# Cross attention in seven products: order of pairs in the second pass, raw buffers, loads two products ahead, and FFN combinations in three steps

## The chip, the core and the metric

The kernel runs on one core of one Trainium2 chip, as one program. The metric is the device time of one execution in microseconds; lower is better. The engines are TensorE (PE, with its weight loads PEld), VectorE (DVE), ScalarE (ACT), GpSimd (POOL) and SyncE (SP), which here issues most of the transfers. POOL issues transfers too.

## The reference

One step of a streaming encoder layer over 2048 prompt rows (16 tiles of 128) and 128 sample rows, model width 1024. Three sub-layers stand in sequence, each with a norm before and after it and its result added to the residual:

- a mixer: 8 heads of chunked band attention and a depthwise convolution side by side, one projection in and one out (`y = concat([att, c]) @ w_out`);
- cross attention: 4 heads of 256 into 256 memory rows (`softmax(q @ mk.T / 16) @ mv @ w_mo`, with `q = h @ w_mq`);
- a SwiGLU FFN: `(silu(h @ w_gate) * (h @ w_up)) @ w_down`, hidden width 2816.

The outputs are the rows of both groups and the new caches. All is computed to float32 accuracy.

## The kernel before, in words

**Precision.** Each float32 operand is split into a rounded part and a rest ("hi" by an ACT cast, "lo" by a subtraction on DVE or POOL), and each product is three matmuls, `hi*hi + hi*lo + lo*hi` (`mm3`, lines 290 to 294; the three lines are L292, L293, L294).

**Stages.** Memory keys and values, input projections, band attention, output projection (`mixout`, with the sample rows' cross attention spread between its matmuls), prompt cross attention (`phase_cross`), gate and up (`gate_up`), down (`down`).

**Cross attention.** The query and key weights are folded into one 1024x1024 matrix f1 (scores = h times f1), and value and output weights into f2. Pass one (q = 0 to 7) multiplies by f1 and takes the softmax, whose rows go to a DRAM array `zs`; pass two (q = 8 to 15) multiplies the `zs` rows by f2. Each q is a pair of row tiles. The two tiles of a pair and the four quarters of the matrix form a 2x2 block product, done in seven products instead of eight, in the order 0, 1, 3, 4, 5, 6, 2. Each product is 12 matmuls of 128x512 into one PSUM bank. Line 1488 stands in the loop over q and the seven products.

For a pair, `left` loads two tiles (of x1 in pass one, normed; of `zs` in pass two) into the two `xt` buffers, `turned` transposes them on TensorE and makes four sums on POOL (L1372 to L1375), `split` makes hi and lo rows (L1380, L1381), and `collect` adds the products into two z tiles (L1445 is the first copy, L1447 to L1458 the sums). The z region holds four tiles, two pairs. In pass one `softmax` follows (L1387 to L1394). In pass two `residual` follows when a tile's sum is ready: x1 is loaded (L1466), the row is normed (L1339 on ACT, L1341 and L1342 on POOL, L1398 on DVE), x1 is added (L1399, POOL) and the result is stored as x2 (L1400). For the first three pairs (group g = 0) the FFN norm follows (L1404) and `combine` (L1410 to L1417): four sums on POOL and four stores to `hn`, the left operands of the FFN's own seven products. These are the "FFN pairs".

`form` loads a half of one of the seven weight combinations into a `raw` buffer (L1327, SP) and splits it (L1330, L1332). The combined quarters are made earlier by `quad` and wait in `comb`. In pass one the loads stand in `form` itself, `AHEAD` products ahead; at q = 7 the same places are filled with f2.

**Gate and up.** `tform` loads `hn` pieces into `nat` buffers (L1537), transposes them (L1540) and splits them (L1542, L1543). `wforms` loads two weight blocks into `wf`, makes four sums on POOL (L1557 to L1560) with results in `s`, and splits seven forms (L1562, L1563). A block of f does seven products of 12 matmuls of 384 columns; there are 22 blocks for each of three groups, and every second block (odd f) ends with `act_forms`, four more POOL sums. In the first group, `natural` prepares the `hn` of the other eight pairs, one pair each in an odd block: two loads, two norms, one `combine`, all in one call. It has six jobs, two for a pair of half height among them.

**Sample rows in the output projection.** `mixout` does 17 tiles; from the third on every second of the eight steps of a tile adds `RATE` to a counter, and for each whole one a step of `cross_sample` is run (65 in all):

```
due += RATE if i >= FROM else 0.0
while due >= 1:
    next(fill, None)
```

**Places.** Tiles are given fixed places in a few big tiles (`sbF`, `sbR`, the PSUM tile; `Region.at`, offsets in KB) and in smaller ones that are released from phase to phase ("flexb" in the profile). A tag with several places rotates through them. Whoever takes a place waits for the last reader of what was there.

**Order.** Each engine and each queue runs its instructions in a fixed order. The framework plans that order in advance (`schedule_with_timeline_sim=True`, line 1841): the program's order gives the priority, raised for the first forms of `gate_up` by `high_priority(offset=HP)`, and a cost model says when an instruction could start. A wait holds up all that stands behind it on its queue.

## Time and profile before

| | us |
|---|---|
| runs | 3067.57, 3067.44, 3058.28 (median 3067.44) |
| profiled execution, its own time | 3062.37 |
| span of the profile | 3060.6 |
| granted TensorE clock, mean | 0.974 |
| TensorE busy | 2933.8 (96%) |
| VectorE busy | 2282.2 (75%) |
| GpSimd busy | 1618.8 (53%) |
| ScalarE busy | 1446.4 (47%) |

Times in the profile are microseconds from the start of the span. A row of a timeline gives the start, the length, the engine, the line, the operation, output and inputs, the count, and in brackets how long the engine had been idle before it and what ended that. "SPq" and "POOLq" are the queues' own instructions. A busy TensorE is not a TensorE at full rate: its granted clock falls when it has stood idle, so work done is better read from the number of matmuls in a stretch.

### The profile page before, as it was taken

Reading aid. Unit: us, or ns where it says so; the run is one execution under the profiler, and the core shown is the slowest. Engines: PE = TensorE matmul, PEld = TensorE weight load, DVE = VectorE, ACT = ScalarE, POOL = GpSimd, SP = SyncE. Lnnn points to the kernel's source line nnn. Section 1 sums busy time; section 2 is a strip of 40 time slices with the busy share of each in tenths; the row PEclk is TensorE's granted clock in tenths of the full one; section 3 lists DMA queues with packets and bytes.
Section 4 is the critical chain, followed back from the end, with each engine's and each line's share of the span. In section 5 each row is a group of like instructions: output and inputs, shape, how many; then the busy total and the mean of one; then the engine's idle time right before and its main releaser. Section 6 shows DMA issues by size and latency. Waiting matters only on the chain.

```text
span 3060.6 us, 46528 instructions
## 1 busy us (share of the span) xinstructions
PE 2933.8 (96%) x16748; PEld 2696.8 (88%) x16748; DVE 2282.2 (75%) x3224; ACT 1446.4 (47%) x2903; POOL 1618.8 (53%) x1488
## 2 busy tenths in 40 slices
PE   9999999999999997999777899999999999999998
PEld 9999999989987886787667899999999999888887
DVE  6686987867775566778567898887878998665666
ACT  5444455668773344555324333443334444433433
POOL 0267595711125435868766765555555776523413
PEclk9999999989999998999888999999999999999999
DMA  7645252654436656545457443354425334766664
GB/s 273 240 148 170 94 180 93 217 204 168 180 121 220 240 194 205 190 145 193 154 185 237 162 149 130 145 179 162 155 105 175 144 139 172 259 198 200 217 231 146
DMA packets 212500, 544.68 MB, mean 178 GB/s; under 512 B 20710, under 2 KB 86126, under 8 KB 203429
## 3 DMA queue, kind: packets, MB, share of 16 engines
q1 hardware_dynamic: 192733, 455.33, 43.7%
q0 software_dynamic: 19536, 86.39, 7.5%
q8 instruction: 131, 2.15, 0.3%
q14 instruction: 100, 0.82, 0.1%
HBM read 393.76 MB, written 158.58 MB: 180 GB/s over the span
## 4 chain that ended last, share of the span: by engine, by line
PE 71%; DVE 7%; POOL 7%; DMA 7%; issue 6%; ACT 2%; SPq 0%; POOLq 0%; DVEq 0%; ACTq 0%
PE psb L294 18%; PE psb L293 18%; PE psb L292 18%; PE psb L300 5%; PE psb L908 2%; PE psb L878 2%; DMA sbf<-in_w_down_dram 2%; PE psb L895 2%; POOL sbf L1685 1%; DVE flexb L1381 1%; DVE sbr L1563 1%; POOL sbf L1399 1%; DMA sbf<-in_w_in_dram 1%; PE psb L1540 1%; PE psb L841 1%
## 5 line engine op out<-in xcount | busy, mean ns | idle before, releaser
L292 PE MATMUL psb<-sbr 128*128 128x384 f32 (+3 forms) x2808 | 942.2, 337 | 11.1 <-DVE sbf L1622 3.7
L293 PE MATMUL psb<-sbr 128*128 128x384 f32 (+3 forms) x2356 | 805.9, 342 | 0.4 <-DVE sbr L342 0.3
L294 PE MATMUL psb<-sbr 128*128 128x512 f32 (+3 forms) x1848 | 634.6, 345 | 3.2 <-DVE sbr L1755 3.1
L292 PEld LDWEIGHTS psb<-sbr 128*128 128x128 f32 x2808 | 530.1, 189 | 41.7 <-DVE sbf L1622 4.1
L294 PE MATMUL psb<-sbr,sbx 128*128 128x384 f32 (+2 forms) x1484 | 475.8, 322 | 0.2 <-POOL sbx L287 0.2
L293 PEld LDWEIGHTS psb<-sbr 128*128 128x128 f32 x2356 | 445.1, 189 | 26.8 <-DVE sbr L342 0.5
L294 PEld LDWEIGHTS psb<-sbr 128*128 128x128 f32 x1848 | 349.0, 189 | 33.0 <-DVE sbr L1755 6.1
L1563 DVE TENSOR_TENSOR sbr<-sbf,sbr 128x512 fp32r<-128x512 f32 x258 | 267.9, 1040 | 40.5 <-ACT sbr L1562 39.0
L1562 ACT CAST sbr<-sbf 128x512 fp32r<-128x512 f32 x258 | 159.3, 620 | 269.6 <-PE psb L293 224.5
L294 PEld LDWEIGHTS psb<-sbr,sbx 128*128 128x128 f32 x1484 | 279.7, 189 | 0.8 <-POOL sbx L287 0.5
L546 DVE SCALAR_TENSOR_TENSOR psb<-sbf,psb 128x768 f32<-128x768 f32 (+1 forms) x290 | 264.4, 912 | 6.1
L1755 DVE TENSOR_TENSOR sbr<-sbf,sbr 128x384 fp32r<-128x384 f32 (+2 forms) x242 | 175.4, 748 | 91.9 <-ACT sbr L1754 90.2
L292 PE MATMUL psb<-sbr,flexb 128*128 128x512 f32 (+2 forms) x528 | 199.8, 379 | 20.6 <-ACT sbf L1445 16.0
L287 POOL TENSOR_TENSOR sbx<-sbf,sbr 128x1024 fp32r<-128x1024 f32 (+1 forms) x62 | 153.0, 2470 | 89.2 <-ACT sbr L285 85.8
L294 PE MATMUL psb<-sbr,flexb 128*128 128x512 f32 (+2 forms) x528 | 198.5, 377 | 0.2 <-DVE flexb L1563 0.2
L1685 POOL TENSOR_TENSOR sbf<-sbf 128x512 f32<-128x512 f32 x77 | 107.7, 1404 | 167.1 <-DMA sbf<-in_w_down_dram 165.4
L293 PE MATMUL psb<-sbr,flexb 128*128 128x512 f32 (+2 forms) x500 | 190.5, 381 | 3.1 <-DVE sbr L1332 2.2
L1754 ACT CAST sbr<-sbf 128x384 fp32r<-128x384 f32 (+2 forms) x242 | 112.5, 483 | 171.2 <-PE psb L293 144.7
L556 POOL TENSOR_TENSOR flexb<-flexb,flexb 128x128 f32<-128x128 f32 (+1 forms) x180 | 168.8, 938 | 25.8 <-ACT flexb L555 15.5
L1562 ACT CAST sbx<-sbf 128x512 fp32r<-128x512 f32 x153 | 94.7, 620 | 177.9 <-PE psb L293 148.0
L1563 DVE TENSOR_TENSOR sbx<-sbf,sbx 128x512 fp32r<-128x512 f32 x153 | 159.2, 1041 | 22.1 <-ACT sbx L1562 21.8
L292 PE MATMUL psb<-sbr,sbx 128*128 128x384 f32 (+1 forms) x524 | 170.8, 328 | 2.5 <-ACT sbr L1542 2.0
(379 smaller groups left out, 6902.1 us busy)
## 6 DMA issues: line engine op xcount, KB each, us to landing
af<-flexb SPq DMA_DIRECT2D x33, 1344.0 KB, 5.9
sbf<-in_w_down_dram SPq DMA_DIRECT2D x154, 256.0 KB, 3.8
sbf<-in_w_gate_dram SPq DMA_DIRECT2D x66, 512.0 KB, 3.3
sbf<-in_w_up_dram SPq DMA_DIRECT2D x66, 512.0 KB, 3.4
sbf<-af SPq DMA_DIRECT2D x85, 384.0 KB, 3.8
sbf<-x SPq DMA_DIRECT2D x51, 512.0 KB, 4.7
sbf<-in_w_in_dram SPq DMA_DIRECT2D x48, 512.0 KB, 3.6
sbr<-ks POOLq DMA_DIRECT2D x16, 1024.0 KB, 7.6
```

What stands on the lines that cost most here:

```text
L287: self.lo_engine.tensor_tensor(lo[:, c], wf[:, c], hi[:, c].bitcast(F32), ALU.subtract)
L292: nc.tensor.matmul(ps, lh, rh, start=start, stop=False, **kw)
L293: nc.tensor.matmul(ps, lh, rl, start=False, stop=False, **kw)
L294: nc.tensor.matmul(ps, ll, rh, start=False, stop=stop, **kw)
L300: nc.tensor.matmul(y[o], l, r[:, o * 512:(o + 1) * 512], start=start and x == 0, stop=stop and x == 2)
L546: nc.vector.scalar_tensor_tensor(acc if w < CW - 1 else o, src(w), cwt[:, j, w:w + 1], acc, ALU.mult, ALU.add)
L556: nc.gpsimd.tensor_tensor(o, o, v, ALU.add)
L1562: nc.scalar.copy(hs[j][:, :], src[j])
L1563: nc.vector.tensor_tensor(ls[j][:, :], src[j], hs[j][:, :].bitcast(F32), ALU.subtract)
L1685: nc.gpsimd.tensor_tensor(acc[:, :], acc[:, :], q[:, :], ALU.add if s > 0 else ALU.subtract)
L1754: nc.scalar.copy(ch[:, m], a[:, x, m])
L1755: nc.vector.tensor_tensor(cl[:, m], a[:, x, m], ch[:, m].bitcast(F32), ALU.subtract)
```

## The change

Constants: `RATE` 1.1 becomes 1.25, `AHEAD` 2 becomes 3, `POOLED` (the products whose second "lo" is made on POOL) loses all of pass one and has three products instead of four in pass two, and `VORDER` gives the order of the pairs in pass two. In `phase_cross` the raw loads leave `form` and are issued two products ahead of it; their places, and those of the PSUM tags, are listed anew; the next pair's `left(1)` stands behind the first forms; the x1 loads of pass two leave `collect` and SP, and are issued on POOL's queue at the fourth product of a pair; the post gain is loaded at the sixth product of q = 7. `natural` becomes a generator with three steps (loads and sums of squares; scaling; combination), of which one runs after each block of the first group, and its places move. `gate_up` gets other places for nearly all its tiles: the weights (`wf`) where the g tiles of cross attention were, `nat` where `xt` was, the forms where the forms of the first products were.

```
-RATE = 1.1
+RATE = 1.25
-AHEAD = 2
-POOLED = ((3, 4, 5, 6, 2), (0, 3, 5, 2))
+AHEAD = 3
+POOLED = ((), (4, 6, 2))
+VORDER = (3, 0, 4, 1, 5, 2, 6, 7)
...
-                .at("raw", 4, (sbF, [16, 20, 24, 28]), *[(a, o) for _ in range(2) for a, o in (
-                    (ft, [0]), (fx, [0]), (sbF, [46.5, 24, 28]))], *[(a, o) for _ in range(5) for a, o in (
-                        (ft, [0]), (fx, [0]), (sbF, [46.5]))])
+                .at("raw", 4, (sbF, [16, 20, 24, 28, 16, 20, 24, 28, 46.5]), (ft, [0]), (sbF, [24, 28]), (fx, [0]), (sbF, [46.5]),
+                    *[(a, o) for _ in range(4) for a, o in ((ft, [0]), (fx, [0]), (sbF, [46.5, 42.5]))])
...
-        ps_mm = ps_t = Region().at("mm", 2, (self.ps, [0, 2, 4, 6])).at("t", 2, (self.ps, [12, 14, 8, 10]))
+        ps_mm = ps_t = Region().at("mm", 2, (self.ps, [2, 6, 0, 4])).at("t", 2, (self.ps, [8, 10, 12, 14]))
+        turn = lambda q: pairs[q] if q < 8 else pairs[VORDER[q - 8]]
...
-        def form(m, j):
+        def raw(m, j):
             out = []
-            for a in range(2):
-                raw = self.t(pool, [P, 2, 512], F32, "raw")
...
+                out.append(self.t(pool, [P, 2, 512], F32, "raw"))
+                nc.sync.dma_start(out[-1][:, :, :], src)
+            return out
+
+        def form(m, j, parts):
+            out = []
+            for a, x in enumerate(parts):
...
-            for t in pairs[q % 8][:2]:
+            for t in turn(q)[:2]:
...
-        late = Region().lay(sbF, 0, ("na", 4, 1), ("nb", 4, 1), ("nt", 4, 1))
-        def natural(g, p):
...
+        late = (Region().at("na", 4, (sbF, [16])).at("nb", 4, (sbF, [20])).at("nt", 4, (sbF, [46.5]))
+                .at("junk", 2, (sbF, [34.5])).lay(sbF, 50.5, ("ss", 0.015625, 6), ("rstd", 0.015625, 6)))
+        def naturals(jobs):
+            for g, p in jobs:
+                n = PAIRS[g][p][2]
+                out = []
+                for tag, (t, r0) in zip(("na", "nb"), PAIRS[g][p][:2]):
+                    x = self.t(late, [P, D], F32, tag)[:n, :]
+                    nc.sync.dma_start(x, self.x2[t][r0:r0 + n, :])
+                    out.append((x, rstd(x, n, late)))
+                yield
+                for x, r in out:
+                    stt(x, x, r[:n, :], gffn[:n, :], ALU.mult, ALU.mult)
+                yield
+                combine(self.hn[g][:, p, :, :], *[x for x, _ in out], self.t(late, [P, 2, 512], F32, "nt")[:n])
+                yield
+        self.todo = naturals([(1, 0), (1, 1), (1, 2), (2, 0), (2, 1), (2, 2)])
...
-                x = self.t(pool, [P, D], F32, "x1")[:, :]
-                nc.sync.dma_start(x, self.x1[t])
+                x = xs.pop((q, "b" if j == 5 else "a"))
                 residual(t, y, x)
...
         nat = left(0)
+        raws = [raw(0, j) for j in order[:2]]
         gs = turned(nat)
         acts = {j: split(*gs[j]) for j in order}
-        nat = left(1)
         f = {}
         for x in range(AHEAD):
-            f[order[x]] = form(0, order[x])
+            f[order[x]] = form(0, order[x], raws.pop(0))
+            raws.append(raw(0, order[x + 2]))
+        nat = left(1)
         for q in range(16):
             for x, j in enumerate(order):
                 if q == 0 and x + AHEAD < 7:
-                    f[order[x + AHEAD]] = form(0, order[x + AHEAD])
+                    f[order[x + AHEAD]] = form(0, order[x + AHEAD], raws.pop(0))
+                    if x + AHEAD + 2 < 7:
+                        raws.append(raw(0, order[x + AHEAD + 2]))
...
+                if q == 6 and x in (2, 4):
+                    raws.append(raw(1, order[x // 2 - 1]))
                 if q == 7:
-                    f[j] = form(1, j)
+                    f[j] = form(1, j, raws.pop(0))
+                    if x + 2 < 7:
+                        raws.append(raw(1, order[x + 2]))
+                    if x == 5:
+                        self.gpost = self.gain(pool, "g_mem_post", "gain")
+                if q > 7 and x == 3:
+                    for t, name in zip(turn(q), "ab"):
+                        xs[q, name] = self.t(pool, [P, D], F32, "x1")[:, :]
+                        nc.gpsimd.dma_start(xs[q, name], self.x1[t])
...
-            if q == 7:
-                self.gpost = self.gain(pool, "g_mem_post", "gain")
...
-        pool = (Region().at("wf", 4, (sbF, [12, 18, 46.5, 22]))
-                .at("s", 2, (sbF, [26, 28, 38.5])).at("nat", 2, (sbF, [40.5, 42.5, 44.5]))
...
+        pool = (Region().at("wf", 4, (sbF, [0, 4, 8, 12]))
+                .at("s", 2, (sbF, [42.5, 44.5, 24])).at("nat", 2, (sbF, [40.5, 38.5, 36.5]))
...
-                .at("wh", 2, (sbR, [68, 72, 76, 80, 84, 88, 92, 104]), (w8, [0]))
+                .at("wh", 2, (sbR, [100, 104, 64, 80, 84, 68, 0, 4]), (w8, [0]))
...
-        for j, (oh, ol) in enumerate(((0, 6), (12, 18), (56, 62), (24, 30), (36, 42), (48, 96))):
+        for j, (oh, ol) in enumerate(((88, 94), (8, 14), (20, 26), (72, 32), (38, 44), (50, 56))):
...
-                    if g == 0 and x == 1 and self.todo:
-                        self.natural(*self.todo.pop(0))
+                    if g == 0:
+                        next(self.todo, None)
```

34 lines of the change are left out of this document (11 added, 23 removed).

## The prediction

> **What bounds the kernel now.** I read the page first, then the busy time by stage, then the idle gaps of TensorE with what ended them, then the rows of the queue that ended each.
>
> ```profile
> PE 2933.8 (96%) x16748; PEld 2696.8 (88%) x16748; DVE 2282.2 (75%) x3224; ACT 1446.4 (47%) x2903; POOL 1618.8 (53%) x1488
> ```
>
> TensorE is the bound over the whole span, so an edit that leaves its instructions alone can only win back time in which it stood or ran slowly. The busy time by stage (start:end, length, PE busy, instructions, granted clock) shows where:
>
> ```profile
> 1187.70:1240.00 52.30, 32.70 (x129) 0.77 0.52 171
> 1240.00:1390.00 150.00, 147.24 (x695) 1.00 0.52 179
> 1390.00:1470.00 80.00, 77.42 (x369) 0.98 0.50 175
> 1470.00:1550.00 80.00, 56.12 (x230) 0.81 0.47 172
> 1550.00:1592.20 42.20, 42.20 (x189) 1.00 0.48 160
> 1592.20:1680.00 87.80, 57.74 (x321) 0.83 0.68 231
> 1680.00:1800.00 120.00, 106.28 (x577) 0.94 0.49 170
> 1800.00:1950.00 150.00, 150.00 (x867) 1.00 0.33 122
> ```
>
> Cross attention runs from 1187.7 to 1592.2, gate and up after it. Undisturbed, a matmul of cross attention costs 0.226 us (42.2 us for 189, four of them transposes) and one of gate/up 0.173 us (150/867). The transposes within the stages, busy time and count:
>
> ```profile
> 1187.70:1240.00 52.30, 6.86 (x44) 0.77 0.52 171
> 1240.00:1390.00 150.00, 13.20 (x100) 1.00 0.52 179
> 1470.00:1550.00 80.00, 6.72 (x37) 0.81 0.47 172
> 1592.20:1680.00 87.80, 15.42 (x88) 0.83 0.68 231
> ```
>
> At 0.132 us each (13.20/100) the full-rate work is: stage A (1187.7 to 1240) 44×0.132 + 85×0.226 = 25.0; stage D (1470 to 1550) 41×0.132 + 189×0.226 = 48.1 (37 transposes and four of the next phase); stage E (1592.2 to 1680) 88×0.132 + 233×0.173 = 51.9; stage F (1680 to 1800) 577×0.173 = 99.8. Lost: **A 27, D 32, E 36, F 20 us**, and some 5 us in the rest of cross attention (150 − 147.24 and 80 − 77.42 idle). Those 120 us are all that the change can reach. The gaps on TensorE, the idle time in brackets:
>
> ```profile
> 1201.16 0.76 PE L292 MATMUL psb<-sbx,flexb 128*128 128x512 f32 x1 [9.00 <-DVE flexb L1081]
> 1475.59 0.79 PE L292 MATMUL psb<-sbr,flexb 128*128 128x512 f32 x1 [5.48 <-ACT sbf L1445]
> 1514.20 0.80 PE L292 MATMUL psb<-sbr,flexb 128*128 128x512 f32 x1 [9.32 <-ACT sbf L1445]
> 1611.23 1.97 PE L1540 MATMUL psb<-ident,sbf 128*128 128x128 f32 x8 [19.02 <-DMA sbf<-hn]
> 1742.70 0.69 PE L292 MATMUL psb<-flexb,sbx 128*128 128x384 f32 x1 [6.31 <-DVE flexb L1613]
> ```
>
> **The change part by part.**
>
> *Start of cross attention (A).* The 9.00 us go to the new PSUM order: the first product now takes the bank of the output projection's last tile but one, not one that L1081 of the last tile still reads. The rest is late raw loads on SP (a row of its queue, and the landing of L1327's loads):
>
> ```profile
> 1215.01 0.90 SPq L1327 DMA_DIRECT2D flexb<-comb  x2
> ...
> DMA to landing us min/median/max: 3.3/3.5/7.2
> ```
>
> The flexb pair at 1215, 27 us into the phase, is the third product's; these two buffers come free only when the last mixer tile is stored. Now the third and fourth products use 16 to 31 KB of the big tile again, and the two flex buffers first serve the second half of the fifth and the seventh. RATE 1.25 finishes the sample stream's 65 steps by step 52 of 60 (1.25×52 = 65) instead of step 60 (1.1×60 = 66), so buffers that the first forms need are free two tiles earlier. The subtractions of pass one leave POOL:
>
> ```profile
> L1332 DVE TENSOR_TENSOR sbr<-sbf,sbr x6: 1214/1220/3378, 1182.4 to 1406.6; 128x1024 fp32r<-128x1024 f32 x6
> L1332 POOL TENSOR_TENSOR sbr<-sbf,sbr x4: 2364/2963/3454, 1184.2 to 1388.2; 128x1024 fp32r<-128x1024 f32 x4
> ```
>
> Five of 2.96 us become five of 1.22 on DVE, 6.1 us more there. What is late next: the flex buffer, and a mixer tail without filler. The chain of the tile before the last shows both (squares, residual sum, store, and the landing of such stores):
>
> ```profile
> 1173.24 0.59 ACT L1077 ACTIVATE flexb<-psb 128x512 bf16<-128x512 f32 x1
> 1178.09 3.31 POOL L1082 TENSOR_TENSOR flexb<-flexb 128x1024 f32<-128x1024 f32 x1 [0.69 <-DVE flexb L1081]
> 1182.60 0.62 POOL L1083 DMA_DIRECT2D x<-flexb  x1
> ...
> DMA to landing us min/median/max: 3.1/5.8/7.9
> ```
>
> From the squares to the residual sum, which follows the last read of PSUM, 4.8 us: with the sample's matmuls gone, two tile boundaries stand open for up to that, 9.6 us; transposes of the first pair can fill some, I take 6. From squares to the store's issue 10 us, landing 3.1 to 5.8; then a raw load of 3.5, a cast of about 1 and a subtraction of 1.2 (its DVE row): the fifth product's second half is ready 19 to 22 us after the tile, needed after 4.5 products of 12×0.226 = 2.7, at 12. That is some 9 us of stall. DVE has two forms of 1.2 a product of 2.7, beside splits and collecting: another 5, an estimate. A costs 20 instead of 27: **7 saved**; bounds −5 (POOL and DVE hold the tile's tail as long as now, and 9.6 of tail less the 5 of forms come on top) and 22 (only the 5 of forms stay).
>
> *Second pass (D).* TensorE waits for ACT's first copy of a pair, which waits for a z buffer, freed when a pair two before is normed and stored. That is late because x1 is late:
>
> ```profile
> 1460.20 31.04 SPq L1355 DMA_DIRECT2D sbf<-zs  x4
> 1491.35 0.36 SPq L1466 DMA_DIRECT2D sbf<-x  x1
> 1495.62 2.40 POOL L1399 TENSOR_TENSOR sbf<-sbf 128x1024 f32<-128x1024 f32 x1 [2.67 <-DMA sbf<-x]
> ```
>
> L1355 stands on SP for buffers that TensorE's transposes free, with x1's load queued behind: 31 us. Now x1 leaves SP for POOL's queue, issued at the fourth product. POOL pays two issues per pair; the nearest row is that of its stores, and beside it stand the other prices of POOL (busy, mean ns):
>
> ```profile
> L1400 POOL DMA_DIRECT2D x<-sbf x16: 533/605/628, 1423.5 to 1608.9; - x16
> ...
> L1342 POOL TENSOR_TENSOR sbf<-sbf,mhalf 128x1 f32<-128x1 f32 x23 | 14.8, 646 | 1.3
> L1373 POOL TENSOR_TENSOR sbf<-sbf 128x512 f32<-128x512 f32 x7 | 10.6, 1511 | 0.3
> L1341 POOL TENSOR_SCALAR sbf<-sbf 128x1 f32<-128x1 f32 x23 | 10.4, 453 | 22.0 <-ACT sbf L1339 21.1
> ```
>
> POOL's work for a pair: four sums of 1.5, two residuals of 2.4, two rstd of 1.1 (0.45 + 0.65), two stores of 0.6: 14.2; an FFN pair adds two rstd, four combinations of 1.5 and four stores: 24.8. TensorE's pair is 84×0.226 + 16×0.132 = 21.1. Three FFN pairs in a row overrun it by 3.7 us each; alternated with plain ones, two pairs with the new issues cost 41.4 of 42.2. So the new order balances POOL, with hardly any slack. What queues behind a waiting x1 load on POOL: the sums of the pair after next, which the splits and then TensorE wait for. An x1 buffer of a plain pair is free only when the FFN pair's combinations have landed, a wait of 3 to 6 us (L1083's landing), three times. So 15 remain of 32: **17 saved**; bounds −76 (the slow rival's price) and 29.
>
> The Trainium skill (SBUF — State Buffer, "SBUF: two separate sides") speaks against this step: a DMA of the GpSimd queue cannot write its descriptors while DVE holds the shared port pair, some 3.1 us in place of 0.62. By that the 16 loads would cost up to 40 us of POOL; the trace disagrees so far, since L1400's 16 issues never exceed 628 ns.
>
> *Loads two ahead, q=6 and 7.* POOL's forms go from four to three; the gap here is 2 us in 1390 to 1470. Nothing taken; −3 to 3.
>
> *Into gate/up (E).* Before, the hn loads wait for the region of the post gain, freed by the last L1398:
>
> ```profile
> 1595.79 1.26 POOL L1414 TENSOR_TENSOR sbf<-sbf 128x512 f32<-128x512 f32 x1
> 1601.27 0.19 POOL L1341 TENSOR_SCALAR sbf<-sbf 128x1 f32<-128x1 f32 x1
> 1604.92 1.28 DVE L1398 SCALAR_TENSOR_TENSOR sbf<-sbf 128x1024 f32<-128x1024 f32 x1
> ```
>
> L1398 ends at 1606.2, 14 us after the last product, about 5 of them because L1341 stands behind a combination burst on POOL. Now hn lands in the old xt buffers and the weights in the g buffers, both idle for most of the last pair, so the first four activation forms are done under it. What is late next: the weight sums (L1557) go into the gain's region. From the last product, an estimate: L1398 ends at about 8 us (14 less POOL's 5 and some), then come two POOL sums of 1.3, a cast and a subtraction of under 1 each: product two starts near 12, while TensorE has 12×0.173 = 2.1 us of product and 36 transposes (4.8). Some 5 us stand open; with DVE and POOL busy and the clock lagging after it (0.83 in this stage) I take 16 left of 36: **20 saved**; bounds 8 (transposes and forms stay late, less than half of the 19 goes) and 32.
>
> *Naturals in three steps (F).*
>
> ```profile
> 1737.78 4.40 DVE L1563 TENSOR_TENSOR sbr<-sbf,sbr 128x512 fp32r<-128x512 f32 x1
> 1737.92 1.27 POOL L1558 TENSOR_TENSOR sbf<-sbf 128x512 f32<-128x512 f32 x1
> ...
> 1740.37 1.26 POOL L1560 TENSOR_TENSOR sbf<-sbf 128x512 f32<-128x512 f32 x1
> ```
>
> One DVE subtraction lasts exactly as long as three POOL sums: POOL's bursts, not DVE's own work, make L1613 late. Today a whole natural (10.6 us of POOL by the prices under D) falls into one block of 84×0.173 = 14.5 us, always an odd one, in which act_forms runs too; then it falls into three blocks, the combination into an odd one only every other time. That burst of 8.4 us remains: **9 of 20 saved**; bounds 0 and 18.
>
> By the Trainium skill (SBUF — State Buffer, "SBUF: two separate sides") the loser of that shared pair is blocked for the other's whole instruction, and the trace agrees (4.40 against three times 1.26). By it a burst of unchanged length costs the same in any block, F would save nothing and the sum would be 9 us less.
>
> *The rest.* The moved regions also change what the down projection can load early; one load of about 4 us (3.5 in L1327's row), hidden by the last block of gate/up of 14.5 or, if not, paid once.
>
> Sum: 7 + 17 + 20 + 9 = 53. The profiled execution took 3062.4 us (span 3060.6), 5 under the median of 3067.4 and within the runs' 3058 to 3068; 3062.4 − 53 = 3009, and I say **3010**.
>
> **The rivals.**
>
> *Only the second half pays:* POOL becomes the bound of pass two and the flex buffer holds the start; A and D give nothing, E and F 29: 3033. For it: POOL's 41.4 of 42.2. Against: SP's 31 us wait is certainly gone.
>
> *Nearly all goes:* the upper bounds, 22 + 29 + 32 + 18 = 101: 2961. Against: the chains named above as late next.
>
> *No change:* the stalls move, as the planned order of each queue differs from the run's; 3055 to 3072. For it: today's raw loads were also planned in time.
>
> *Slower:* POOL stands at x1's loads. They are early in its order and wait for the previous pair's stores, and all its sums wait behind. Then D's 17 turn into a loss; the other parts give 36, so it decides from 36/8 = 4.5 us a pair above today's stalls. If each pair waits 9.5 us (two rstd prices, L1398, L1399 and a store's landing of 3.1 to 5.8, an estimate), eight cost 76: 3062 − 36 + 76 = 3102. For it: SP shows today exactly this fault, 31 us long. Against: the load is issued at the fourth product, when a plain pair's residuals are done. The Trainium skill's descriptor rule, cited under D, would act at the same place.
>
> **How the numbers follow.** Forecast (2985 to 3030) 0.55; second half only 0.19; nearly all 0.13; no change 0.07; slower 0.06. The range 2975 to 3058 leaves out the slow case, most of no change and about half of "nearly all". With 0.3% (9 us) as what a measurement tells from nothing: faster 0.87, same 0.07, slower 0.06.
>
> **What would show it.** A: no gap before L1081, the third product's raw loads from the big tile before 1190, a stall at the fifth product instead. D: no x1 load on SP; L1399 not waiting for DMA; gaps before L1445 of at most 15 us in all. E: TensorE's gap after the last product under 6 us, ended by a weight form. F: the 100 us after that at near 0.173 us a matmul. Wrong: POOL standing over 5 us at x1's loads while TensorE idles, or more than 10 us of new gaps in the last two mixer tiles.

## The result and the profile after

The changed kernel takes 3044.27 us (median of five runs, 3040.77 to 3046.68), the kernel before 3067.44 (five runs, 3058.28 to 3071.50); the ratio is 0.9932, 95% interval 0.9912 to 0.9953. It is faster by 0.7%, some 21 us. The profiled executions differ by 15.7 us (3062.37 and 3046.68, spans 3060.6 and 3044.9). The forecast was 3010, a gain of 53 on the profiled execution. Line numbers from here on are those of the changed kernel, 1 to 20 above those of before; where a row is of the kernel before, the text says so.

The busy time of the changed kernel, from its page, and its stretches at the stage bounds of the prediction (start:end, length, PE busy, instructions, granted clock, DMA share, GB/s):

```profile
PE 2935.2 (96%) x16748; PEld 2700.2 (89%) x16748; DVE 2293.1 (75%) x3230; ACT 1442.9 (47%) x2903; POOL 1601.8 (53%) x1498
```

```profile
1187.70:1240.00 52.30, 44.36 (x188) 0.90 0.61 216
...
1470.00:1550.00 80.00, 73.82 (x342) 0.98 0.51 183
1550.00:1592.20 42.20, 38.08 (x181) 0.94 0.61 209
1592.20:1680.00 87.80, 68.55 (x358) 0.87 0.60 218
1680.00:1800.00 120.00, 102.90 (x557) 0.96 0.50 174
1800.00:1950.00 150.00, 150.00 (x867) 1.00 0.31 119
```

The first row looks like a win over before (44.36 us busy against 32.70), but part of it is mixer work that was done earlier before. Windows of fixed time mix stages once work moves, so I read the stages between events that both kernels have: the first matmul of the output projection (L301), the first copies of the second, the ninth and the sixteenth pair (L1454), and the last x1 copy (L1619) of group 0 that comes one undisturbed block of 14.56 us after the one before. I call the four stretches A (mixer and start of cross attention), B (first pass), D (second pass), EF (into gate and up, and group 0). In us:

| | A | B | D | EF | sum |
|---|---|---|---|---|---|
| before | 341.8 | 161.0 | 177.3 | 390.6 | 1070.7 |
| changed | 343.0 | 161.0 | 166.5 | 384.9 | 1055.3 |
| changed, profiled again (e16) | 344.6 | 158.7 | 163.8 | 385.9 | 1053.1 |

The two executions of the changed kernel differ by up to 2.7 us in a stretch. From kernel to kernel a stretch moves more, since an edit also shifts the planned order elsewhere: in eight executions with RATE 1.25 whose edits lie behind the mixer, A is 339.8 to 345.9, and in e1, whose edit lies in the mixer, EF is 11.2 shorter. So a few us in one stretch of two kernels are little evidence, and I lean on groups of runs where I can. The gain of the profiled pair is 10.8 in D and 5.7 in EF; A lost 1.2, B is equal. The forecast was 7 in A, nothing in B, 17 in D and 29 in EF.

TensorE's largest gaps now (idle time and its end in brackets):

```profile
997.35 3.06 PE L301 MATMUL psb<-sbr,sbx 128*128 128x512 f32 x7 [3.28 <-DVE flexb L1082]
1046.31 2.79 PE L1195 MATMUL psb<-ident,sbf 128*128 128x128 f32 x12 [2.56 <-DVE flexb L1033]
1192.03 0.79 PE L293 MATMUL psb<-sbx,flexb 128*128 128x512 f32 x1 [8.51 <-ACT flexb L1385]
1223.42 0.79 PE L294 MATMUL psb<-flexb,flexb 128*128 128x512 f32 x1 [3.58 <-DVE flexb L1337]
1419.25 0.80 PE L293 MATMUL psb<-sbx,flexb 128*128 128x512 f32 x1 [5.37 <-DVE sbf L1461]
1597.67 1.09 PE L1560 MATMUL psb<-ident,sbf 128*128 128x128 f32 x4 [3.93 <-DMA sbf<-hn]
1668.76 0.69 PE L293 MATMUL psb<-sbr 128*128 128x384 f32 x1 [4.91 <-DVE sbf L1622]
1702.19 0.69 PE L293 MATMUL psb<-flexb,sbr 128*128 128x384 f32 x1 [5.80 <-DVE sbf L1633]
```

The waits of 9.00, 5.48, 9.32 and 19.02 us are gone. In their place stand a wait of 8.51 for the first split rows, two gaps in the mixer that were not there, and waits for DVE in gate and up.

### The profile page after: what moved, and what is told of

It is laid out like the page before. It is cut to its first block, busy times and chain, and to the rows that moved or that the text cites. A ratio compares the mean times of both kernels' runs of the same rounds, so it can differ in the third digit from the quotient of the medians.

```text
span 3044.9 us, 46489 instructions
## 1 busy us (share of the span) xinstructions
PE 2935.2 (96%) x16748; PEld 2700.2 (89%) x16748; DVE 2293.1 (75%) x3230; ACT 1442.9 (47%) x2903; POOL 1601.8 (53%) x1498
## 3 DMA queue, kind: packets, MB, share of 16 engines
q8 instruction: 131, 2.15, 0.3%
## 5 line engine op out<-in xcount | busy, mean ns | idle before, releaser
L293 PE MATMUL psb<-sbr 128*128 128x384 f32 (+3 forms) x2796 | 938.2, 337 | 11.3 <-DVE sbf L1622 6.4
L294 PE MATMUL psb<-sbr 128*128 128x384 f32 (+3 forms) x2492 | 850.1, 341 | 0.1
L293 PEld LDWEIGHTS psb<-sbr 128*128 128x128 f32 x2796 | 528.0, 189 | 42.5 <-DVE sbf L1622 7.3
L294 PEld LDWEIGHTS psb<-sbr 128*128 128x128 f32 x2492 | 470.8, 189 | 26.4 <-DVE sbr L343 0.4
L295 PE MATMUL psb<-sbr,sbx 128*128 128x384 f32 (+2 forms) x1260 | 404.2, 321 | 0.1
L295 PEld LDWEIGHTS psb<-sbr 128*128 128x128 f32 x1836 | 346.7, 189 | 32.4 <-DVE sbr L1775 5.6
L1583 DVE TENSOR_TENSOR sbr<-sbf,sbr 128x512 fp32r<-128x512 f32 x307 | 337.8, 1102 | 38.8 <-ACT sbr L1582 38.1
L1582 ACT CAST sbr<-sbf 128x512 fp32r<-128x512 f32 x307 | 189.8, 620 | 321.3 <-PE psb L294 281.1
L295 PEld LDWEIGHTS psb<-sbr,sbx 128*128 128x128 f32 x1260 | 238.5, 189 | 0.8 <-DVE sbx L1583 0.6
L1705 POOL TENSOR_TENSOR sbf<-sbf 128x512 f32<-128x512 f32 x77 | 106.7, 1391 | 167.2 <-DMA sbf<-in_w_down_dram 164.5
L293 PE MATMUL psb<-sbr,flexb 128*128 128x512 f32 (+2 forms) x500 | 188.4, 377 | 4.4 <-ACT sbf L1454 3.2
L294 PE MATMUL psb<-sbr,flexb 128*128 128x512 f32 (+2 forms) x500 | 187.8, 376 | 0.0
L295 PE MATMUL psb<-sbr,flexb 128*128 128x512 f32 (+2 forms) x500 | 187.1, 375 | 0.0
L557 POOL TENSOR_TENSOR flexb<-flexb,flexb 128x128 f32<-128x128 f32 (+1 forms) x180 | 168.5, 937 | 26.1 <-ACT flexb L556 15.7
L1577 POOL TENSOR_TENSOR sbf<-sbf 128x512 f32<-128x512 f32 x66 | 97.8, 1483 | 99.1 <-DVE sbr L1583 58.5
L294 PE MATMUL psb<-sbx,sbr 128*128 128x256 f32 (+3 forms) x480 | 146.7, 306 | 0.0
L286 ACT CAST sbr<-sbf 128x1024 fp32r<-128x1024 f32 x98 | 102.4, 1050 | 92.3 <-PE psb L294 43.2
```

What stands on the lines that cost most here:

```text
L286: nc.scalar.copy(hi[:, :], wf[:, :])
L293: nc.tensor.matmul(ps, lh, rh, start=start, stop=False, **kw)
L294: nc.tensor.matmul(ps, lh, rl, start=False, stop=False, **kw)
L295: nc.tensor.matmul(ps, ll, rh, start=False, stop=stop, **kw)
L557: nc.gpsimd.tensor_tensor(o, o, v, ALU.add)
L1582: nc.scalar.copy(hs[j][:, :], src[j])
```

## The experiments

All eighteen in one table. The ratios are to the kernel before, run on the same chip at the same time; the runs stand on five chips, so ratios are compared and not medians.

| run | median us | ratio, 95% interval | A | B | D | EF |
|---|---|---|---|---|---|---|
| e1 RATE 1.1 | 3028.68 | 0.9872 (0.9858–0.9887) | 331.4 | 163.9 | 165.5 | 373.7 |
| e2 before, RATE 1.25 | 3077.14 | 1.0034 (1.0021–1.0047) | 352.9 | 161.7 | 175.3 | 396.6 |
| e3 combination in one step | 3044.83 | 0.9924 (0.9911–0.9938) | 345.4 | 160.1 | 162.8 | 387.2 |
| e4 its sums on DVE | 3029.67 | 0.9873 (0.9854–0.9891) | 340.9 | 160.9 | 167.3 | 367.4 |
| e5 e1 and e4 | 3035.53 | 0.9885 (0.9864–0.9906) | 331.6 | 166.4 | 162.6 | 379.3 |
| e6 RATE 1.25, cross held back | 3049.72 | 0.9930 (0.9918–0.9942) | 343.4 | 165.7 | 168.0 | 387.4 |
| e7 old places of gate and up | 3057.56 | 0.9948 (0.9933–0.9963) | 345.9 | 160.0 | 166.2 | 393.6 |
| e8 old order of pairs | 3052.02 | 0.9938 (0.9921–0.9955) | 339.8 | 161.4 | 186.6 | 364.3 |
| e9 x1 on SP | 3028.62 | 0.9861 (0.9839–0.9883) | 340.8 | 160.1 | 159.6 | 377.3 |
| e10 RATE 1.1, order 0,3,1,4,2 | 3058.47 | 0.9959 (0.9944–0.9974) | 335.1 | 164.9 | 188.0 | 376.0 |
| e11 e10, sums on DVE | 3031.24 | 0.9874 (0.9850–0.9897) | 332.8 | 166.9 | 188.0 | 353.2 |
| e12 e11, act_forms on DVE | 3035.46 | 0.9884 (0.9863–0.9905) | 329.2 | 165.1 | 189.2 | 356.2 |
| e13 e1 and e9 | 3024.62 | 0.9849 (0.9834–0.9864) | 334.0 | 166.2 | 160.0 | 378.4 |
| e14 e13, sums on DVE | 3017.82 | 0.9830 (0.9812–0.9847) | 333.1 | 163.4 | 160.9 | 373.5 |
| e15 e14, old order of pairs | 3025.45 | 0.9854 (0.9837–0.9870) | 333.4 | 163.8 | 177.3 | 360.7 |
| e16 changed kernel again | 3044.53 | 0.9915 (0.9901–0.9930) | 344.6 | 158.7 | 163.8 | 385.9 |
| e17 sums in even blocks | 3037.66 | 0.9894 (0.9878–0.9911) | 340.3 | 157.2 | 163.7 | 384.1 |
| e18 e14, sums in even blocks | 3017.80 | 0.9832 (0.9817–0.9846) | 333.2 | 165.1 | 161.0 | 371.6 |

**The mixer (e1, e2, e6).** e1 puts back one constant; e2 changes it alone in the kernel before.

```
e1, in the changed kernel        e2, in the kernel before
-RATE = 1.25                     -RATE = 1.1
+RATE = 1.1                      +RATE = 1.25
```

> The changed kernel with RATE 1.1 instead of 1.25, nothing else. Theory 1 (the mixer lost what the start won): with 1.25 TensorE's order holds cross attention's first 16 transposes and two of its matmuls ahead of the last 72 mixer matmuls, and the mixer's last matmul ends at 1212.2 instead of 1187.7. With 1.1 the order has the mixer's matmuls first again: the last one ends before 1196, no gap of over 5 us stands between the first transposes and the second product, the second pair's first copy (1238.6 now) comes 10 to 18 us earlier, and the time is 10 to 18 us below the changed kernel's 3044. Rival a (the raw loads decide): the sample stream ends later, its buffers free the raw loads later, the start stall of some 9 us comes back and the time is within 5 us of 3044. Rival b (only a lower clock in that profile): the mixer ends where it likes and the time is within 3 us of 3044.

> The kernel before with RATE 1.25 instead of 1.1, nothing else. Theory 1: the sample stream runs out eight steps early, the last mixer tiles stand without other work and gaps open earlier in the mixer too, so it is slower than before by 5 to 15 us (3072 to 3082), with the last mixer matmul after 1195 instead of 1187.7. Rival a: the earlier freed buffers let the first forms come earlier, the stall before the first product shrinks, and it is 3 to 9 us faster than before.

RATE 1.25 is slower in both kernels, as theory 1 said. A falls by 11.6 us with 1.1 and rises by 11.1 with 1.25 in the old kernel; e1 is 0.4 to 0.6% faster than the changed kernel, e2 0.3% slower than before. The groups don't overlap: with the new cross attention, A is 329.2 to 335.1 in nine profiles with 1.1 and 339.8 to 345.9 in nine with 1.25. One sign of e1 failed: a wait of over 5 us (5.91) does stand before its first product. TensorE's last mixer work in the changed kernel and in e1 (timeline):

```profile
1177.38 4.38 PE L301 MATMUL psb<-sbr,sbx 128*128 128x512 f32 x18
1181.61 1.91 PE L1373 MATMUL psb<-ident,sbf 128*128 128x128 f32 x16
1192.03 0.79 PE L293 MATMUL psb<-sbx,flexb 128*128 128x512 f32 x1 [8.51 <-ACT flexb L1385]
1192.62 0.63 PE L294 MATMUL psb<-sbr,flexb 128*128 128x512 f32 x1
1193.28 6.86 PE L301 MATMUL psb<-sbr,sbx 128*128 128x512 f32 x24
...
1206.77 5.61 PE L301 MATMUL psb<-sbr 128*128 128x512 f32 x24
```

```profile
1178.00 2.89 PE L301 MATMUL psb<-sbr 128*128 128x512 f32 x12
1180.72 1.03 PE L1373 MATMUL psb<-ident,sbf 128*128 128x128 f32 x8
...
1189.68 0.79 PE L293 MATMUL psb<-sbx,flexb 128*128 128x512 f32 x1 [5.91 <-ACT flexb L1385]
```

With RATE 1.25 the last 72 matmuls of the output projection stand behind cross attention's transposes and the 8.51 us that its first product waits; but e1 waits there too, 5.91 us here and 2.86 at 1205.65. e6 keeps 1.25 and takes that order away:

```
 (mm3h keeps its last matmul as self.last_mm)
-        gs = turned(nat)
+        with self.tc.issue_after(self.last_mm.ins):
+            gs = turned(nat)
```

> The changed kernel with RATE 1.25 kept, but cross attention's first transposes issued after the last mixer matmul. It splits theory 1 in two. If TensorE's order alone costs the 15.6 us of RATE 1.25, the time falls to 3026 to 3033 as with 1.1. If the mixer tail without other work costs them (two tile boundaries wait for the eviction of the tile before, and the gaps of 3.28 and 2.56 us near 997 and 1046 stay), it stays within 5 of 3044, and the last mixer matmul still ends after 1203. In between, as I expect: gaps of 5 to 9 us before the last tiles' first matmuls, the last mixer matmul at 1198 to 1206, the time 3034 to 3040.

It gained nothing: A is 343.4 as in the changed kernel, the time 3049.7, outside the 3034 to 3040 that I expected. The mixer's order is whole again, but the last tiles wait for their banks (e6, timeline), as in e2:

```profile
1183.48 7.26 PE L301 MATMUL psb<-sbr,sbx 128*128 128x512 f32 x24 [7.62 <-DVE flexb L1082]
```

```profile
1187.99 7.35 PE L300 MATMUL psb<-sbr,sbx 128*128 128x512 f32 x24 [9.20 <-DVE flexb L1081]
```

So the order of the tail is not the price: TensorE waits there in either order. The price lies earlier. To 1100 and to 1178, just before the first wait of the tail, the kernel before and then the changed one, which start that stretch within 0.3 us of each other, do this:

```profile
895.80:1100.00 204.20, 199.59 (x1042) 0.98 0.61 210
895.80:1178.00 282.20, 277.21 (x1448) 0.99 0.61 210
```

```profile
895.80:1100.00 204.20, 195.18 (x1006) 0.95 0.59 204
895.80:1178.00 282.20, 272.33 (x1400) 0.96 0.60 206
```

36 instructions fewer at 0.19 us (199.59/1042) are 7 us, 48 are 9 of the 11 to 12. In the first 282.2 us of the stretch the kernels with 1.1 do 1445 (e1) and 1448, those with 1.25 do 1400 (the changed kernel, twice), 1407 (e6) and 1409 (e2). The sample work is not missing there: its last split on DVE ends at 1170.4 in the changed kernel and at 1176.7 before. So it is the denser stream that costs most of it. The gaps near 997 and 1046 and the lower clock behind them stand in that stretch; e2 has gaps of 3.50 and 2.46 at the same two places. In front of the first one POOL has put two small steps of the tile's norm between the sums of `quad` (changed kernel; L310 and L311 are the norm's, L1082 on DVE waits for them):

```profile
989.19 1.61 POOL L1272 TENSOR_TENSOR sbf<-sbf 128x512 f32<-128x512 f32 x1 [5.96 <-DMA sbf<-f1s]
...
992.29 1.28 POOL L1272 TENSOR_TENSOR sbf<-sbf 128x512 f32<-128x512 f32 x1 [1.34 <-DMA sbf<-f1s]
993.66 0.18 POOL L310 TENSOR_SCALAR flexb<-flexb 128x1 f32<-128x1 f32 x1
...
995.94 0.57 POOL L311 TENSOR_TENSOR flexb<-flexb,mhalf 128x1 f32<-128x1 f32 x1
```

So this gap came about on POOL. Why the planned order is so, and what else the denser stream costs, was not taken apart.

**The FFN combinations of gate and up (e3, e4, e17).**

```
e3                                     e17
-   if g == 0:                         -   if g == 0:
-       next(self.todo, None)          -       next(self.todo, None)
+   if g == 0 and x == 1:              +   if g == 0 and f:
+       for _ in range(3):             +       for _ in range(1 + x):
+           next(self.todo, None)      +           next(self.todo, None)

e4
-        def combine(dst, xa, xb, u):
+        def combine(dst, xa, xb, u, pt=ptt):
-            ptt(u[:, 0, :], xb[:, 0, :], xa[:, 0, :], ALU.subtract)   (and three more)
+            pt(u[:, 0, :], xb[:, 0, :], xa[:, 0, :], ALU.subtract)
-  combine(self.hn[g][:, p, :, :], ..., "nt")[:n])
+  combine(self.hn[g][:, p, :, :], ..., "nt")[:n], tt)
```

> The changed kernel with each FFN combination of gate and up put back into one block, every second one, instead of three steps in three blocks. Theory 3 (the steps buy nothing, since the burst of four POOL sums and the sums after it stay together, and DVE stands through each of them): time within 4 us of the changed kernel's 3044; TensorE's loss over its last 155 us before 1800 (155 less 708 times 0.173, 32 us now) stays within 6. The prediction's own claim: the loss grows by some 9 us and the time rises to about 3053. Rival c (three steps are worse, as the two stages in numbers say: 160 less 790 times 0.173, 23 us before, against 32 now): the time falls by 6 to 10 us.

> The changed kernel with the four sums of each of the six FFN combinations of gate and up on DVE instead of POOL; the stores stay on POOL's queue. Theory 3 (POOL's unbroken sums hold DVE up, which makes TensorE's banks late): 24 sums of about 1.6 us leave POOL, and DVE takes 24 of 0.7 to 1.0; the gaps of 4.91 before L1622 and 5.80 before L1633 go, and the time falls by 8 to 20 us against the changed kernel's 3044. Rival d (DVE's own amount of work decides): DVE has 17 to 24 us more in that stage, and the time rises by 3 to 15 us.

> The changed kernel with each FFN combination of gate and up in two blocks instead of three steps in three: loads, squares and scaling in the odd block, which act_forms ends, the four sums in the even one, always away from act_forms; POOL does the same work. Theory 3 (the length of POOL's bursts decides): from the sixteenth first copy to the end of group 0's copies 370 to 378 us instead of 385, and the ratio to before falls from 0.9915 to 0.987 to 0.990. Rival (any block is as bad, what counts is the sum of POOL's work beside DVE): within 4 us of 385.

e3 is the changed kernel to within the noise (0.9924 against 0.9932 and 0.9915): the three steps bought nothing. e17's EF is within 2 us of e16; its time is 0.2% lower, but the profile has that in A (4.3), which the edit does not touch. The reason is the planned order: the place in the program moves, the place on the queue hardly does. In e17 the last sum (L1421) and the first of act_forms (L1673 there) still stand 2.4 us apart, as in the changed kernel (1688.43 and 1690.83):

```profile
1681.39 1.29 POOL L1421 TENSOR_TENSOR sbf<-sbf 128x512 f32<-128x512 f32 x1
1683.79 1.40 POOL L1673 TENSOR_TENSOR flexb<-flexb 128x384 f32<-128x384 f32 x1 [1.11 <-DVE flexb L1647]
```

It is so at all six combinations. From the start of the last sum to the start of the next act_forms, in us:

| | 1 | 2 | 3 | 4 | 5 | 6 |
|---|---|---|---|---|---|---|
| changed, e3 and e17, alike | 31.7 | 1.9 | 2.4 | 3.0 | 9.9 | 14.2 |
| e7 (old places) | 53.8 | 15.6 | 17.3 | 11.7 | 10.0 | 15.5 |
| before | 77.2 | 41.2 | 11.8 | 16.4 | 18.2 | 12.9 |

So neither e3 nor e17 tried the separation that they were meant to try. And before, no act_forms followed a combination closely; the new places of gate and up brought them together, as e7 shows.

What a burst does is seen in the changed kernel, POOL and then DVE, in front of the gap of 5.80 at 1702:

```profile
1693.30 1.30 POOL L1577 TENSOR_TENSOR sbf<-sbf 128x512 f32<-128x512 f32 x1
1694.54 1.01 POOL L1673 TENSOR_TENSOR flexb<-flexb 128x384 f32<-128x384 f32 x1
...
1698.91 0.98 POOL L1675 TENSOR_TENSOR flexb<-flexb 128x384 f32<-128x384 f32 x1
1699.87 1.25 POOL L1580 TENSOR_TENSOR sbf<-sbf 128x512 f32<-128x512 f32 x1
```

```profile
1693.16 0.54 DVE L1630 TENSOR_TENSOR sbf<-sbf,psb 128x384 f32<-128x384 f32 x1
1693.62 8.05 DVE L1583 TENSOR_TENSOR sbr<-sbf,sbr 128x512 fp32r<-128x512 f32 x1
1701.59 0.54 DVE L1633 TENSOR_TENSOR sbf<-sbf,psb 128x384 f32<-128x384 f32 x1
```

One subtraction of at best 0.67 us stands for 8.05, under seven sums without a break, and the eviction L1633 behind it frees TensorE's bank that much later. The longest one before was 4.72 (DVE):

```profile
1696.25 4.72 DVE L1563 TENSOR_TENSOR sbr<-sbf,sbr 128x512 fp32r<-128x512 f32 x1 [2.62 <-ACT sbr L1562]
```

e4 takes the sums off POOL, and the same subtractions (groups of DVE from 1600 to 1800, changed kernel and e4) get shorter:

```profile
L1583 DVE TENSOR_TENSOR sbr<-sbf,sbr 128x512 fp32r<-128x512 f32 x50 | 76.8, 1541 | 4.4 <-ACT sbr L1582 4.3
```

```profile
L1583 DVE TENSOR_TENSOR sbr<-sbf,sbr 128x512 fp32r<-128x512 f32 x56 | 57.6, 1038 | 4.8 <-ACT sbr L1582 4.7
```

More of these subtractions take less time, the gaps of 4.91 and 5.80 are gone (the longest from 1620 to 1840 is 3.87), and EF falls by 17.5 us. Rival d, by which the time rises, falls in this kernel.

**Do the two gains add? (e5)** The edits of e1 and of e4 together.

> The changed kernel with RATE 1.1 and with the four sums of each of the six FFN combinations of gate and up on DVE. If the two faults are separate, their gains add up: 15.6 for RATE (3044.3 to 3028.7) and 14.6 for the sums (3044.3 to 3029.7), 3044.3 less 30 is 3014, 3010 to 3018. If one hides behind the other (the later start of gate and up meets the same bursts), it stays at 3024 to 3030.

No: 3035.5 (3026.6 to 3046.8), by ratio 0.9885, not below e1's 0.9872. A kept its 11 us, EF came out 5.6 above e1. In e5 one scaling (the row of L1438 on DVE, 1600 to 1800: shortest, median and longest ns) met seven sums of act_forms and the weights:

```profile
L1438 DVE SCALAR_TENSOR_TENSOR sbf<-sbf,flexb x10: 1269/1281/8677, 1622.2 to 1745.4; 128x1024 f32<-128x1024 f32 x8, 64x1024 f32<-64x1024 f32 x2
```

**The places of gate and up (e7).**

```
-        pool = (Region().at("wf", 4, (sbF, [0, 4, 8, 12]))
-                .at("s", 2, (sbF, [42.5, 44.5, 24])).at("nat", 2, (sbF, [40.5, 38.5, 36.5]))
+        pool = (Region().at("wf", 4, (sbF, [12, 18, 46.5, 22]))
+                .at("s", 2, (sbF, [26, 28, 38.5])).at("nat", 2, (sbF, [40.5, 42.5, 44.5]))
...
-        late = (Region().at("na", 4, (sbF, [16])).at("nb", 4, (sbF, [20])).at("nt", 4, (sbF, [46.5]))
+        late = (Region().lay(sbF, 0, ("na", 4, 1), ("nb", 4, 1), ("nt", 4, 1)).at("junk", 2, (sbF, [16]))
```

> The changed kernel with the regions of gate and up (weights, sums, activations, and the combinations' tiles) as before, nothing else. The prediction's E: the gap of some 19 us behind cross attention comes back and the time rises by 15 to 25, to 3059 to 3069. Theory 4 (the new places only cut one gap of 19 into several that add up to nearly as much: 3.93 and 2.92 and six of 1 to 2 us in 1590 to 1620, at a clock of 0.58 to 0.83): the time rises by 3 to 8 only. If the new places are themselves what makes the later blocks worse, the time does not rise.

EF is 8.7 above the changed kernel, by ratio 0.2 to 0.3%: between the prediction's 20 and theory 4's 3 to 8, nearer to the latter. The interval of e7 overlaps the one of the result (0.9912 to 0.9953) and lies above that of e16, so the worth is only roughly known. The old wait is back, with a gap on TensorE of 16.67 us at 1598.31, as this list of SP's waits shows for e7, and it is another one in the changed kernel (1540 to 1620, both; waits in all, times, longest):

```profile
SPq L1557 <- DVE sbf L1403: 30.8, 1, 30.8
```

```profile
SPq L1557 <- PE psb L1560: 19.7, 13, 6.0
SPq L1557 <- DMA hn<-sbf: 12.9, 2, 12.7
```

With the new places the hn loads no longer wait for the residual's gain but for the store of hn by the last FFN pair, and that comes later than before because of the new order of the pairs.

**The order of the pairs and the queue of x1 (e8, e9, e10, e15).**

```
e8   -VORDER = (3, 0, 4, 1, 5, 2, 6, 7)
     +VORDER = (0, 1, 2, 3, 4, 5, 6, 7)
e9   -                        nc.gpsimd.dma_start(xs[q, name], self.x1[t])
     +                        nc.sync.dma_start(xs[q, name], self.x1[t])
e10  RATE = 1.1 and VORDER = (0, 3, 1, 4, 2, 5, 6, 7)
e15  RATE = 1.1, x1 on nc.sync, sums on DVE (all as e14) and VORDER = (0, ..., 7)
```

> The changed kernel with the pairs of the second pass in the order of before (the three pairs with an FFN combination first, one after another), nothing else. The prediction's reading of D (POOL overruns TensorE by 3.7 us on each of three FFN pairs in a row): the second pass from the ninth first copy to the sixteenth grows from 166.5 us by 8 to 14, and the time rises by as much, unless the earlier freed POOL at the end of the pass gives some back in gate and up. Rival: POOL has enough room and the time stays within 4 of 3044, then all of D's gain of 11 comes from the x1 loads alone.

> The changed kernel with the loads of x1 for the residuals back on SP's queue, at the same point of the program (the fourth product). With e8 it splits D. If the queue mattered (x1 stood behind the loads of L1356, which wait for buffers), the second pass from the ninth first copy to the sixteenth grows from 166.5 us by 6 to 12, POOL's L1404 waits for x1 longer than the 3.71 and 4.09 us of now, and the ratio to before rises from 0.993 to 0.995 to 0.997. If the order of the pairs alone gave D, the pass stays within 3 us of 166.5 and the ratio within 0.0015 of 0.993.

> The changed kernel with RATE 1.1 and the pairs of the second pass in the order 0, 3, 1, 4, 2, 5, 6, 7: FFN pairs still alternate with plain ones, but each comes one pair (21 us) earlier. Theory 5 (what the new order wins in the second pass it gives back behind it, because the last FFN combination and with it the loads of hn come later): the second pass stays within 4 us of the 165.5 of e1, the time from the sixteenth first copy to the first x1 copy of gate and up falls from 49 us towards the 36 of e8, by 5 to 12, and the ratio to before falls from e1's 0.9872 to 0.983 to 0.986. Rival (hn waits for the buffers of the last pair's loads, whatever the order): those 49 us stay within 3 and the ratio within 0.002 of 0.987.

> As e14, but the pairs of the second pass in the order of before (0 to 7, the FFN pairs first). If the order of the pairs decides the second pass (a plain pair behind an FFN pair waits for its x1 buffer until the combination is stored): the pass takes 178 to 188 us as in e8 and e10, and gate and up wins 10 to 20 back, as the FFN pairs are done early. If the queue of the loads decided: the pass takes 158 to 168.

The steps of D are clearest in the time from one pair's first copy to the next one's (21.1 us undisturbed), here up to the pair named on top, with the pairs that do an FFN combination:

| | FFN pairs | 9 | 10 | 11 | 12 | 13 | 14 | 15 |
|---|---|---|---|---|---|---|---|---|
| before | 8, 9, 10 | 23.5 | 16.8 | 36.0 | 38.6 | 29.1 | 14.1 | 19.2 |
| e8 | 8, 9, 10 | 24.9 | 24.7 | 35.7 | 36.9 | 31.4 | 13.7 | 19.2 |
| e15 | 8, 9, 10 | 23.9 | 19.1 | 35.3 | 38.0 | 26.9 | 14.8 | 19.2 |
| e10 | 8, 10, 12 | 24.9 | 25.8 | 31.1 | 21.4 | 32.7 | 15.9 | 36.2 |
| changed | 9, 11, 13 | 25.2 | 24.3 | 27.0 | 25.6 | 15.4 | 30.4 | 18.6 |
| e9 | 9, 11, 13 | 23.9 | 22.2 | 20.6 | 25.2 | 23.1 | 25.2 | 19.4 |

With FFN pairs at q, the first copy of q + 3 is late: 11, 12, 13 in the first three rows, 11, 13, 15 in e10, 12 and 14 in e9, whose third one would be 16, behind the pass. In the changed kernel only 14 (30.4) stands out by these times, but 12 waited as well: ACT stood 6.69 us for the store of x2 that frees the z tile.

```profile
1501.61 0.59 ACT L1454 COPY sbf<-psb 128x512 f32<-128x512 f32 x1 [6.69 <-DMA x<-sbf]
```

The chain that fits: the two x1 buffers of the FFN pair are free only when its combination is stored, the pair behind it is normed and stored late, and the pair two further on waits for its z tile. Its middle in the changed kernel (POOL's timeline): the last store of the combination, the next pair's x1 loads, their landing.

```profile
1478.87 0.61 POOL L1422 DMA_DIRECT2D hn<-sbf  x1
...
1482.52 0.59 POOL L1518 DMA_DIRECT2D flexb<-x  x1
1483.11 0.54 POOL L1518 DMA_DIRECT2D sbf<-x  x1
1483.66 1.29 POOL L1380 TENSOR_TENSOR sbf<-sbf 128x512 f32<-128x512 f32 x1
1486.27 2.68 POOL L1404 TENSOR_TENSOR sbf<-sbf,flexb 128x1024 f32<-128x1024 f32 x1 [1.32 <-DMA flexb<-x]
```

The order, all else equal: e15 against e14, 177.3 and 160.9, 16.4 us; e8 against the changed kernel 20.1, more than the 8 to 14 that I expected. In e15, with x1 on SP at the fourth product, D is what it was before (177.3), so the order alone won what D won. The loads come no earlier there: for the second and third pair of the pass 54.8 and 93.1 us after its start, 54.1 and 92.7 before. What SP waits for at them is the store of the combination, as the chain says (e15, 1395 to 1580; waits in all, times, longest):

```profile
SPq L1518 <- DMA hn<-flexb: 49.7, 3, 24.8
```

Theory 5 of e10 failed in its first half, and usefully: FFN pairs that alternate but begin the pass are as bad (188.0) as three in a row (186.6), so POOL's balance over two pairs is not the cause. Its second half came true beyond its size (the time to gate and up's first copy falls from 49.3 us to 26.2), yet EF as a whole is 2.3 us longer than in e1. The queue: with x1 back on SP the pass is 6.9 us shorter (e9), 5.5 in e13 against e1, and with the old order 9.3 (e15 against e8, which differ in RATE and in the sums too). In nine profiles with the new order and x1 on POOL the pass takes 162.6 to 168.0, in four with x1 on SP 159.6 to 161.0: POOL's queue cost some 5 us. POOL did not stand at the loads (0.5 us idle before all sixteen); they stood behind its other work. The pair of loads in the rows above comes 9.4 and 4.2 us after the last store out of its buffer is issued (L1420 and L1422), in e9 3.6 and 2.5. The gap of 5.37 at the ninth pair's start is 2.15 in e9. e9's expectation was wrong in sign.

What the order wins in D it gives back in EF, all or most of it: 20.6 us (e8 against changed) and 12.8 (e15 against e14). In e8 the hn loads (SP's waits, 1550 to 1630) no longer wait for a store:

```profile
SPq L1557 <- PE psb L1560: 29.1, 18, 4.9
SPq L1557 <- PE psb L1373: 20.8, 1, 20.8
```

By ratio e8 and the changed kernel can't be told apart (0.9938; 0.9932 and 0.9915).

**The parts put together (e11 to e14, e18, e16).** e11 is e10 with e4's edit, e13 e1 with e9's, e14 e13 with e4's, e18 e14 with e17's; e16 is the changed kernel. e12 adds to e11:

```
-        tt = nc.gpsimd.tensor_tensor
+        tt = (nc.vector if g == 0 else nc.gpsimd).tensor_tensor      (in act_forms)
```

> As e10, and the four sums of each of the six FFN combinations of gate and up on DVE, as in e4. In e5 these gave nothing on top of RATE 1.1: one DVE scaling of 1.28 us stood for 8.68 us under seven POOL sums in a row there. If it is chance which DVE instruction meets a burst, e11 lies within 8 us of e10 on either side; if the sums on DVE help as in e4, it is 8 to 15 us faster than e10.

> As e11, and in group 0 the four sums of act_forms on DVE too, so that POOL's longest burst in these blocks is the four weight sums, some 5 us, in place of 8.7. Theory 3 (the length of POOL's unbroken bursts makes TensorE's banks late): no DVE instruction of group 0 lasts over 5.5 us, gaps before gate and up's products stay under 3 us, and it is 4 to 12 us faster than e11. Rival (DVE's own work, 26 of 29 us per two blocks then, decides): it is 3 to 10 us slower than e11.

> The changed kernel with RATE 1.1 and the loads of x1 on SP's queue (e1 and e9 together). If their gains add (20.9 and 17.6 of profile, of which 11 and 7 in different stages): ratio to before 0.981 to 0.984, some 3015 to 3020; from the first mixer matmul to the second pair's first copy 330 to 334 us, the second pass 158 to 162. If the later stages give it back: 0.986 to 0.988.

> As e13, and the four sums of each of the six FFN combinations of gate and up on DVE. If bursts of POOL cost as in e4 against the changed kernel and e11 against e10 (17 and 23 us from the sixteenth first copy to the end of group 0): 8 to 17 us faster than e13, ratio 0.976 to 0.981. If chance decides as in e5: within 6 us of e13.

> As e14 (RATE 1.1, x1 on SP, the sums of the combinations on DVE), with the sums in the even blocks as in e17. With no POOL sums in the combinations any more, the place should matter little: within 5 us of e14's 3018, ratio 0.981 to 0.985; if act_forms and DVE's four sums collide in the odd blocks, 5 to 10 us faster.

> The changed kernel as it is, on the chip of the three others: ratio to before 0.991 to 0.995, as in the result (0.9932), with the last mixer matmul 316 us after the first and the second pass at 163 to 168 us. If it lies outside, ratios of different chips can't be compared to 0.002.

e11 is 22.8 us below e10 in EF, so the sums on DVE help there; e14 is 4.9 below e13, at the edge of what can be told, and in e5 they cost. Across four pairs of kernels that is −17.5, −22.8, −4.9 and +5.6: mostly a gain, its size a matter of which DVE instruction meets which burst. Nor does a long wait of DVE have to cost: e14 has a scaling of 9.19 us. e12 shows that a shorter burst is not enough: no subtraction of L1583 lasts over 3.35 us there (8.05 in the changed kernel), yet EF is no shorter than in e11 (3.0 longer), and the time is 4 us longer, as its rival said (by ratio within the noise). That DVE's own amount of work then counts is a guess; no run took it apart. e13 adds e1 and e9 only in A and D (334.0 and 160.0); EF gives 6.5, less than e1 (11.2) or e9 (7.6) had alone, so the ratio lies between the two that were expected. e14, at 3017.8, is the fastest with e18, 1.7% below before and 27 us below the changed kernel on the same chip (e16). e18 shows no difference of place.

## Why the prediction was right or wrong, step by step

Direction and range held (2975 to 3058); the size did not, 15.7 of 53 on the profiled executions. None of the four rivals is what happened. Set against e8, which lacks only the new order, the loss has one main place. With the old order, EF is 26.3 us below before (364.3), near the 29 that E and F were to give, though not by F's way, and D is 9.3 above (186.6). The new order then wins 20.1 in D and costs 20.6 in EF. The other loss is the 11 us of RATE in A. These are single profiles, so each figure is good to a few us.

**A, 7 forecast, −1.2 measured.** The step that failed is "two tile boundaries stand open for up to that, 9.6 us; ... I take 6". It put the price of RATE 1.25 at the tail, where sample work is missing. The price is 11 to 12 us (e1, e2), and 7 to 9 of them are lost before the tail, while the denser sample work still runs. The prediction has no term for them. The waits of the tail, 8.51 us here, are matched by 8.77 in e1. With RATE 1.1 the rest of A is a gain of 10.4 (341.8 to 331.4 in e1), less 2.9 that pass one then loses. That this comes near the 7 of the forecast is luck: the 7 had 6 us of tail and 9 of a stall taken off that did not come. The gap before L1081 went, as said. The stall at the fifth product did not come; a shorter one came in the fourth (3.58 at 1223.42).

**D, 17 forecast, 10.8 to 13.5 measured.** Mechanism and price were both partly wrong. "So the new order balances POOL" is refuted by e10. The sentence that "an x1 buffer of a plain pair is free only when the FFN pair's combinations have landed" named the true cause, but sized it at 3 to 6 us; the late copies cost 8 to 17 each before. Leaving SP was taken for the heart of the gain; it cost some 5 us. The 31 us that x1's load stood on SP were not the limit: in e15 it is placed earlier, waits for the combination's store, and is issued when it was before. That the parts still came to more than half of the 17 is luck, a larger gain by the order less a loss by the queue. The slow rival's "POOL stands at x1's loads" did not happen (0.5 us); the residual stood for their landing instead. The signs: the addition of x1 (L1399, now L1404) waits for the loads six times, 15.6 us in all, against three times and 7.9 us before, where the prediction said "L1399 not waiting for DMA"; the gaps before the first copy are well under 15.

**E, 20 forecast.** The new places are worth 8.7 by profile (e7), which has the old gap again. The gap behind the last product is under 6 us, as said, but it is the hn loads that end it (3.93) and not a weight form. The step that failed is the list of what is late next: it held the weight sums, but not the combination of the third FFN pair, which the new order had put three pairs later (13 instead of 10). D and E were costed as separate terms although one edit, the order, moves the same store from one to the other. Nor were E and F separate: the new places brought the combinations' sums next to act_forms.

**F, 9 forecast, 0 measured** (e3). The lower bound was right, and so was the sentence by the Trainium skill that "by it a burst of unchanged length costs the same in any block" and F saves nothing. The Trainium skill (SBUF — State Buffer, "SBUF: two separate sides") calls the pair of ports that DVE and GpSimd share an exclusive lock, held for a whole instruction; this trace agrees and shows more, one subtraction held for seven sums in a row (8.05 us). The step that failed is "then it falls into three blocks": the planned order put the sums at the same distances from act_forms wherever the program had them. And the sums of before did not run into the next act_forms, from which 11.8 us or more kept them. The stage itself got worse: from 1680 to 1800, 557 matmuls against 577, 3.5 us at 0.173. The same section of the Trainium skill says that DVE can keep a POOL-queue transfer from writing its descriptors; the trace does not show it for these loads, as L1518's sixteen issues took 527 to 617 ns.

**The rest** was nothing, as said: after group 0 both kernels take the same (1094.0 and 1093.9 us to the end of the span).

## What to carry to other kernels

When filler work is packed more densely to end it earlier, price the stretch in which it is denser, and not only the tail that is left without it: here 7 to 9 of 11 us, in each of two kernels. When an edit only reorders jobs, follow the late one past the end of the stage: the order of the pairs won 16 to 20 us in one stage and gave 13 to 21 back in the next. And when one edit of two can shift the planned order of the other's stage, test them apart, in more than one kernel. A place in the program is not a place on the queue; read the written order of the engine before a gain is booked for spreading work.
